# Attention with heads in pairs, a spread and masked forget-gate bias, and attention steps inside the query units, in a float32 decoder of two layers

## The chip, the cores and the metric

The kernel runs on one core of a Trainium2 chip. The metric is the device time of one execution in microseconds (us). The engines are named as the profile names them: PE (matmuls and transpositions; PEld loads its weights), DVE (vector), ACT (scalar, activations), POOL (general) and SP (here only a queue of DMAs).

## The reference, cut to what matters

The model has two layers on 256 tokens of width 1024. Each layer is a half-step feed-forward block (hidden width 2816), a token mixer and a second half-step block. The mixer of layer 0 is a gated linear recurrence, that of layer 1 is attention with a forget gate: keys, values and the gate's running sum `c` come from the stream after layer 0, and there are 16 heads of 64.

```python
kv = (hn @ w_kv).reshape(Bn, S, 2, N_HEADS, HEAD_DIM)
log_f = jax.nn.log_sigmoid((hn @ w_f + b_f).astype(jnp.float32))
c = jnp.cumsum(log_f, axis=1).transpose(0, 2, 1)
...
logits = jnp.einsum('bhqd,bhkd->bhqk', q[:, :, q0:end], k[:, :, :end]).astype(jnp.float32)
logits = logits + c[:, :, q0:end, None] - c[:, :, None, :end]
logits = jnp.where(kpos[None, :] <= qpos[:, None], logits, -jnp.inf)
p = jax.nn.softmax(logits, axis=-1).astype(v.dtype)
outs.append(jnp.einsum('bhqk,bhkd->bhqd', p, v[:, :, :end]))
...
return o @ w_o
```

## The kernel before, in words

**Tokens and weights.** The 256 tokens are two token tiles (t = 0, 1) of 128. Each float32 weight arrives by a DMA on SP's queue as a unit of 128x1024 in one of five `raw` buffers. ACT copies its upper part into `whi` (L199) and DVE subtracts to get the lower part `wlo` (L200). A product is the sum of three matmuls: upper by upper, upper by lower, lower by upper. Either the tokens are stationary and 512 weight columns stream (`mm3`, lines L207, L208, L209), or the weights are stationary and the tokens stream (`mmj`): one matmul of 512 columns, the upper and lower tokens side by side (L222), and one of 256 (L223).

**The order.** PE's instructions run in the order in which the program writes them. The program is a list of items, each with a preparation (load and split) and a piece of work; `slot` runs one, and `tick`, in the middle of each, starts preparations and the calls that `defer(n, fn)` has put off by n ticks. The instructions of ACT, DVE, POOL and SP are put in order by a scheduler, and those traced inside `tc.high_priority()` come ahead of others.

**Banks.** PSUM has eight banks of 512 columns: 0 to 3 for sums ("mm"), 4 and 5 ("gt"), 6 and 7 for transpositions ("tr"). A tile with stationary weights borrows four banks for its eight rows of k (`lent`), in units of two rows (`still`, k0 = 0, 2, 4, 6). At its end `total` and the functions beside it read the four banks (ACT L549, DVE L550).

**Small transpositions.** Gains and parameters are loaded as rows and transposed on PE by deferred calls: `grow` (40 rows, L157) and `prow` (88 rows, L699), each inside a weight-stationary tile of the first feed-forward block.

**K and V.** After layer 0 `v_items` computes V, and `proj_items` K, both with tokens stationary, between 502 and 552 us. `heads_T` (L1010) scales a half of K (`htok`), puts one more column or two behind the 64 of each head (a one and the negative running sum `nck`), and transposes it head by head to `kT` in groups of four heads (L1026), so that a head has 66 rows. Q is treated alike, with the running sum `cq` and a one: the product of the 66 rows then contains the bias of the forget gate. `running` computes the running sums with a triangular matrix.

**Attention.** The string `ATT_ORDER` writes the order of the stage that begins at 736 us: "0" and "1" stand for a unit of token tile 0 or 1 (eight of Q's projection, then eight of the out-projection by `w_o`), "a0" and "a1" for an attention step. A step i has four parts. `logits(i)`: the products of a group of heads (four for t = 0, two for t = 1) into a "gt" bank (L1128), the causal mask added on the diagonal block (L1129), the negative maximum (L1131), and one exponential per head with its sum (L1136). `values(i-3)`: the transposed probabilities `pT` are stationary and 64 columns of `v` stream (L1155). `turn(i-2)`: four transpositions of the probabilities `pe` (L1144), copied to `pT` (L1146). `output`: when eight heads are complete, they are scaled by the inverse sums to `ot` (L1160), transposed (L1168), and split in an upper part `oh` (L1171) and a lower part `ol` (L1172), the stationary operands of the out-projection.

**The end of a token tile.** When the sums of the out-projection are complete, `enter` squares and adds (ACT `junk`, L236), POOL computes the inverse root (L229, L231), and DVE scales by the gain `gb` (L302) and adds to the stream `h` (L306).

## Time and profile before

| | us |
|---|---|
| runs: lowest, median, highest of 3 | 1008.15, 1009.94, 1010.61 |
| the profiled execution's own time | 1007.29 |
| its span in the trace | 1005.6 |
| PE busy | 991.0 (99%) |
| DVE, ACT, POOL busy | 665.3, 566.1, 51.5 |
| projection of V and K | 502 to 552 |
| Q projection, attention, out-projection | 736 to 815 |

The span is the time from the first to the last instruction in the trace. In rows of a timeline the first number is the start and the second the duration; the ends of matmuls are modelled, so what a matmul costs is read from the starts of neighbours. "x4" is a run of four like instructions. In square brackets stands the idle time of the engine ahead of the instruction, and what ended it. In a group the numbers behind the bar are the busy time in us, the mean in ns and the idle time in us.

### The profile page before, as it was taken

How to read it: one execution, taken by the hardware profiler on the slowest of the kernel's cores; microseconds unless marked ns; L12 is line 12 of the kernel's file. 1: busy time of each engine (PE TensorE's matmuls, PEld its weight loads, DVE VectorE, ACT ScalarE, POOL GpSimd, SP SyncE). 2: the span in 40 equal slices, each digit the busy share in tenths (PEclk: the TensorE clock that was granted, in tenths of full speed). 3: DMA queues.
4: the chain of work that ended last, by engine and by line, in shares of the span. 5: the costliest groups of instructions: out<-in, count | busy, mean ns of one | idle time of the engine just before them, and what ended most of it. 6: DMA issues, size and time to landing. Idle time of an engine off the chain costs nothing.

```text
span 1005.6 us, 13910 instructions
## 1 busy us (share of the span) xinstructions
PE 991.0 (99%) x5302; PEld 847.3 (84%) x5302; DVE 665.3 (66%) x768; ACT 566.1 (56%) x742; POOL 51.5 (5%) x113
## 2 busy tenths in 40 slices
PE   8999999999999999999999999999999999999997
PEld 5887888889988888888898888888888888888885
DVE  5877664568998676664695577674477477666642
ACT  5656543559987555543565555553468566555431
POOL 1500000000003000000000000000020020000000
PEclk9999999999999999999999999999999999999999
DMA  6877656565427666545476766655555057665431
GB/s 230 280 263 204 190 161 197 154 181 151 141 78 250 212 188 187 188 158 185 114 227 218 209 191 184 192 189 168 168 168 168 2 188 237 184 199 195 155 121 42
DMA packets 91864, 178.90 MB, mean 178 GB/s; under 512 B 11790, under 2 KB 31318, under 8 KB 91798
## 3 DMA queue, kind: packets, MB, share of 16 engines
q1 hardware_dynamic: 90550, 176.89, 56.8%
q10 hardware_dynamic: 608, 1.06, 0.3%
q8 instruction: 41, 0.67, 0.3%
q0 software_dynamic: 640, 0.07, 0.1%
q14 instruction: 25, 0.20, 0.1%
HBM read 176.95 MB, written 1.05 MB: 177 GB/s over the span
## 4 chain that ended last, share of the span: by engine, by line
PE 70%; issue 21%; ACT 4%; DVE 4%; POOL 1%; DMA 0%; DVEq 0%; POOLq 0%; ACTq 0%
PE pall L222 21%; PE pall L223 11%; PE pall L209 10%; PE pall L208 10%; PE pall L207 10%; PE pall L845 1%; DVE wlo L200 1%; PE pall L214 1%; PE pall L215 1%; PE pall L216 1%; PE pall L1128 1%; ACT junk L236 1%; PE pall L1155 1%; ACT whi L199 1%; PE pall L1026 1%
## 5 line engine op out<-in xcount | busy, mean ns | idle before, releaser
L200 DVE TENSOR_TENSOR wlo<-raw,whi 128x1024 fp32r<-128x1024 f32 (+4 forms) x329 | 394.6, 1206 | 242.3 <-ACT whi L199 241.8
L199 ACT ACTIVATE whi<-raw 128x1024 fp32r<-128x1024 f32 (+4 forms) x329 | 342.1, 1044 | 290.3 <-PE pall L209 125.6
L222 PE MATMUL pall<-xall,whi 128*128 128x512 f32 x1216 | 424.7, 395 | 0.0
L223 PE MATMUL pall<-xall,wlo 128*128 128x256 f32 x1216 | 338.4, 278 | 0.0
L222 PEld LDWEIGHTS pall<-xall,whi 128*128 128x128 f32 x1216 | 228.1, 188 | 53.3
L223 PEld LDWEIGHTS pall<-xall,wlo 128*128 128x128 f32 x1216 | 228.8, 188 | 0.2
L207 PE MATMUL pall<-whi,hhi 128*128 128x512 f32 (+2 forms) x432 | 166.0, 384 | 0.0
L209 PE MATMUL pall<-whi,hlo 128*128 128x512 f32 (+2 forms) x432 | 165.0, 382 | 0.0
L208 PE MATMUL pall<-wlo,hhi 128*128 128x512 f32 (+2 forms) x432 | 164.8, 382 | 0.0
L209 PEld LDWEIGHTS pall<-whi,hlo 128*128 128x128 f32 x432 | 81.1, 188 | 15.1
L208 PEld LDWEIGHTS pall<-wlo,hhi 128*128 128x128 f32 x432 | 81.2, 188 | 14.7
L207 PEld LDWEIGHTS pall<-whi,hhi 128*128 128x128 f32 x432 | 81.2, 188 | 14.6
L207 PE MATMUL pall<-whi,xall 128*128 128x512 f32 (+2 forms) x168 | 67.1, 400 | 0.1
L208 PE MATMUL pall<-wlo,xall 128*128 128x512 f32 (+2 forms) x168 | 64.9, 386 | 0.4 <-DVE wlo L1226 0.2
L209 PE MATMUL pall<-whi,xall 128*128 128x512 f32 (+2 forms) x168 | 64.9, 386 | 0.1
L229 POOL TENSOR_SCALAR nv<-ss 128x1 f32<-128x1 f32 x24 | 10.9, 453 | 749.8 <-ACT junk L236 749.6
L208 PEld LDWEIGHTS pall<-wlo,xall 128*128 128x128 f32 x168 | 31.7, 189 | 7.5 <-DVE wlo L200 1.2
L209 PEld LDWEIGHTS pall<-whi,xall 128*128 128x128 f32 x168 | 31.5, 188 | 7.1 <-DVE xall L259 1.1
L207 PEld LDWEIGHTS pall<-whi,xall 128*128 128x128 f32 x168 | 31.6, 188 | 5.7 <-ACT xall L254 0.5
L567 ACT ACTIVATE hhi<-prod 128x1024 fp32r<-128x1024 f32 (+1 forms) x21 | 20.6, 980 | 25.2 <-DVE prod L563 25.2
L300 DVE SCALAR_TENSOR_TENSOR t<-pall,rstd,gb 128x512 f32<-128x512 f32 x16 | 11.9, 748 | 26.7 <-ACT junk L236 26.7
L557 ACT ACTIVATE sil<-sil 128x1024 f32<-128x1024 f32 (+1 forms) x21 | 20.6, 982 | 15.1 <-DVE sil L556 15.0
(190 smaller groups left out, 974.2 us busy)
## 6 DMA issues: line engine op xcount, KB each, us to landing
raw<-in_ffn_w_down_dram SPq DMA_DIRECT2D x88, 512.0 KB
raw<-in_ffn_w_up_dram SPq DMA_DIRECT2D x80, 512.0 KB
raw<-in_ffn_w_gate_dram SPq DMA_DIRECT2D x79, 512.0 KB
raw<-in_rg_w_in_dram SPq DMA_DIRECT2D x20, 504.0 KB
raw<-in_rg_w_out_dram SPq DMA_DIRECT2D x10, 504.0 KB
raw<-in_ffn_w_gate_dram SPq DMA_DIRECT2D x18, 256.0 KB
raw<-in_ffn_w_up_dram SPq DMA_DIRECT2D x16, 256.0 KB
raw<-in_w_kv_dram SPq DMA_DIRECT2D x8, 512.0 KB
```

Source lines behind the costliest of these rows:

```text
L199: nc.scalar.activation(hi[:parts, c:c + m], rawv[:, c:c + m], AF.Copy)
L200: nc.vector.tensor_tensor(lo[:parts, c:c + m], rawv[:, c:c + m], hi[:parts, c:c + m].bitcast(F32), ALU.subtract)
L207: nc.tensor.matmul(ps, xh, wh, start=first, stop=False)
L208: nc.tensor.matmul(ps, xh, wl, start=False, stop=False)
L209: nc.tensor.matmul(ps, xl, wh, start=False, stop=last)
L214: nc.tensor.matmul(ps, wh, xh, start=first, stop=False)
L222: nc.tensor.matmul(pall[:, b, :], wh, xall[:, k, :, :].rearrange("p a b -> p (a b)"), start=k == 0, stop=False)
L223: nc.tensor.matmul(pall[:, b, :S], wl, xhi[:, k, :], start=False, stop=k == 7)
L229: nc.gpsimd.tensor_scalar(v, ss[:, 0:1], ss[:, 1:2] if n == 2 else 0.0, D * EPS * f * f, ALU.add, ALU.add)
L300: nc.vector.scalar_tensor_tensor(t1[n], pf[n], r_in, gb[:, n * 512:(n + 1) * 512], ALU.mult, ALU.mult)
L557: nc.scalar.activation(s, s, AF.Silu)
L567: nc.scalar.activation(hv, pv, AF.Copy)
```

## The change

**K** becomes a weight-stationary product: `still`, `tile_items` and `total` move to the top level and take the streaming operand as an argument, and the upper and lower halves of `hid` become one tile so that both can stream as one operand. K comes out transposed; its eight groups of transpositions are gone, and a product with the tokens' inverse roots takes their place. `kT` is now [128, 8, 256]: two heads of 64 rows below each other.

**The forget gate** leaves the 66 rows. `nck` is transposed once per token tile (two small transpositions), written to DRAM (`ckd`), and read back by two broadcast loads on SP's queue, `nb0` (1.05 MB) and `nb1` (2.10 MB), to all 128 partitions. POOL writes the causal mask into each (`affine_select` over 2048 elements of a partition). DVE adds this bias to the whole 128x512 logits instead of the mask on the diagonal block.

**The attention step** runs values, turn, logits in this order. Logits use 64 rows of the array per head, the two heads of a pair in its two halves, into two banks. The probabilities are scaled by the inverse sums before they are transposed (one product of 128x512 per group). In `values`, `v` is stationary (64 columns) and 128 columns of `pT` stream; the two heads of a pair write the two halves of the partitions, so the result is transposed already, and `oh` and `ol` are read from it; `ot` and `output` are gone. The vector and scalar operations of the logits stand in `tc.high_priority()`. Q is transposed in four groups of pairs instead of eight of single heads.

**Deferred calls** marked `calm` wait while a weight-stationary tile is in its first or last unit (`state["edge"]`); `ATT_ORDER` is new.

PE at the transposition of `prow`, in the first feed-forward block (`xall` the tokens, `whi` and `wlo` the parts of a weight unit, whose number is that of the build), before:

```order
L222 MATMUL pall<-xall,whi_626 128x512
L223 MATMUL pall<-xall,wlo_627 128x256
L699 MATMUL pall<-ident,prow 126x88
L222 MATMUL pall<-xall,whi_626 128x512
L223 MATMUL pall<-xall,wlo_627 128x256
```

and PE at the same transposition in the changed kernel:

```order
L232 MATMUL pall<-xall,whi_647 128x512
L233 MATMUL pall<-xall,wlo_648 128x256
L712 MATMUL pall<-ident,prow 126x88
L232 MATMUL pall<-xall,whi_647 128x512
L233 MATMUL pall<-xall,wlo_648 128x256
```

It stood behind eight pairs of the first unit of a tile (rows k0 = 0) and stands behind eight pairs of the next unit (k0 = 2), sixteen matmuls later.

PE at the first out-projection unit of token tile 1 (`oh`, `ol` the upper and lower part of the attention's output), before:

```order
L1155 MATMUL pall<-v_2925,pT_6989 128x64
L1155 MATMUL pall<-v_2926,pT_6989 128x64
L1155 MATMUL pall<-v_2925,pT_6989 128x64
L1155 MATMUL pall<-v_2926,pT_6989 128x64
L1144 MATMUL pall<-ident,pe_6962 128x128 x4
L207 MATMUL pall<-whi_6463,oh_6475 128x512
L208 MATMUL pall<-wlo_6464,oh_6475 128x512
L209 MATMUL pall<-whi_6463,ol_6477 128x512
```

and PE there in the changed kernel:

```order
L1202 MATMUL pall<-pT_6904,v_2928 64x128 x2
L1202 MATMUL pall<-pT_6904,v_2929 64x128 x2
L1187 MATMUL pall<-ident,pe_6891 128x128 x4
L1162 MATMUL pall<-kT,qT_6466 128x256 x2
L207 MATMUL pall<-whi_6447,oh_6469 128x512
L208 MATMUL pall<-wlo_6448,oh_6469 128x512
L209 MATMUL pall<-whi_6447,ol_6471 128x512
```

A group of logits has moved from ahead of the values to behind the turn, and the unit follows it; the group's values read the pair's probabilities as streaming operand.

DVE in the changed kernel at the same place: the end of token tile 0 (`t`, `h`) and the logits and `ol` of token tile 1 (`nb` the bias, `mx` the maximum, `sm` the sums):

```order
L312 TENSOR_TENSOR t_1097_6934<-pall,gb_6611 128x512
L1180 RECIPROCAL sm_6911<-sm_6911 128x2
L1181 TENSOR_TENSOR pe_6912<-pe_6912,sm_6911 128x512
L312 TENSOR_TENSOR t_1098_6936<-pall,gb_6611 128x512
L316 SCALAR_TENSOR_TENSOR h_73<-t_1097_6934,rstd_6940,h_73 128x512
L1170 TENSOR_TENSOR pall<-pall,nb_6460 128x2x256
L316 SCALAR_TENSOR_TENSOR h_73<-t_1098_6936,rstd_6940,h_73 128x512
L1172 TENSOR_REDUCE mx_6959<-pall 128x2
L1209 TENSOR_TENSOR ol_6471<-pall,oh_6469 128x512
```

The subtraction that makes the first `ol` of token tile 1, which PE's L209 above reads, stands behind both additions to `h` and a group's bias and maximum.

SP's queue in the changed kernel, ahead of and in the attention stage:

```order
L184 DMA raw_6412<-in_attn_w_q_dram 128x2x512
L187 DMA raw_6445<-in_attn_w_o_dram 128x1024
L187 DMA raw_6594<-in_attn_w_o_dram 128x1024
L187 DMA raw_6613<-in_attn_w_o_dram 128x1024
L1133 DMA nb_6455<-ckd 128x16x128
L1133 DMA nb_6460<-ckd 128x4096
L362 DMA gb_6611<-in_mix_post_g_dram 128x1024
L187 DMA raw_6625<-in_attn_w_o_dram 128x1024
L187 DMA raw_6660<-in_attn_w_o_dram 128x1024
L187 DMA raw_6672<-in_attn_w_o_dram 128x1024
```

The two loads of the bias are new and stand ahead of the gain and of the fourth unit of `w_o`; before, four units of `w_o` stood ahead of the gain and nothing between them.

The diff, cut to its core (in the attention, lines of before that fall away stand in the kernel above):

```diff
-    def defer(n, fn):
-        pend.append([n, fn])
+    def defer(n, fn, calm=False):
+        pend.append([n, fn, calm])
 
     def tick():
         for p in list(pend):
             p[0] -= 1
-            if p[0] < 0:
+            if p[0] < 0 and not (p[2] and state["edge"]):
...
+    def total(v, b, m):
+
+        nc.scalar.activation(v, pall[:, b:b + m, S:], AF.Copy)
+        nc.vector.tensor_tensor(v, pall[:, b:b + m, :S], v, ALU.add)
+
+    def still(u, k0, b0, moving=x_moving):
+        if k0 == 0:
+            assert not set(held) & set(range(b0, b0 + 4)), held.keys()
+            lent.update(range(b0, b0 + 4))
+        state["edge"] = k0 in (0, 6)
+        for j in range(2):
+            for b in range(4):
+                o = j * 512 + b * P
+                mmj(b0 + b, u.hi[:, o:o + P], u.lo[:, o:o + P], k0 + j, moving)
+            if j == 0:
+                tick()
+        if k0 == 6:
+            lent.difference_update(range(b0, b0 + 4))
+            state["edge"] = True
...
-        defer(5, lambda: gains_T(grow, 40, 16))
+        defer(5, lambda: gains_T(grow, 40, 16), True)
...
+    def heads_T(pool, ps, t, n, scale, dst):
+
+        tok = pool.tile([P, 512], F32, tag="htok", name=nm("htok"), bufs=2)
+        nc.vector.tensor_scalar(tok, ps, rs[t][:, 0:1], scale, ALU.mult, ALU.mult)
+
+        def turn():
+            tp = bank("mm")
             for j in range(4):
-                nc.tensor.transpose(tp[:HA, j * P:(j + 1) * P], tok[:, 4 * b + j, :], ident)
-            nc.scalar.activation(dst[:, 8 * n + 4 * b:8 * n + 4 * b + 4, :],
-                                 tp[:HA, :].rearrange("p (a b) -> p a b", a=4), AF.Copy)
-        defer(2, lambda: turn(0))
-        defer(3, lambda: turn(1))
+                nc.tensor.transpose(tp[:, j * P:(j + 1) * P], tok[:, j * P:(j + 1) * P], ident)
+            nc.scalar.activation(dst[:, 4 * n:4 * n + 4, :].rearrange("p a b -> p (a b)"), tp, AF.Copy)
+        defer(2, turn)
 
     def post_k(n):
-        return lambda t, ps: heads_T(pools["f"], ps, t, n, 1.0, (None, kv["nck"][t]), kv["kT"][:, :, t * P:(t + 1) * P])
+        def f(b, m):
+            kk = pools["f"].tile([P, 16 * HA], F32, tag="prod", name=nm("kk"), bufs=1)[:, :1024]
+            v = kk.rearrange("p (a b) -> p a b", a=4)
+            total(v, b, m)
+            nc.vector.tensor_tensor(kv["kT"][:, 4 * n:4 * n + 4, :], v, rcp["v"].unsqueeze(1).to_broadcast([P, 4, S]), ALU.mult)
+        return f
+
+    def z_moving(k):
+        return kv["z"][:, :, :, k, :], kv["z"][:, 0, :, k, :]
...
+    def rows(t):
+        pc = sparebank()
+        nc.tensor.transpose(pc[:NH, :P], kv["nck"][t], ident)
+        nc.vector.tensor_copy(kv["ckT"][:, t * P:(t + 1) * P], pc[:NH, :P])
+        if t == 1:
+            nc.sync.dma_start(kv["dram"], kv["ckT"])
...
-        proj_items(A["w_kv"], n * 512, 512, z_x, post_k(n))
+        tile_items(A["w_kv"], n * 512, 4 - 4 * n, post_k(n), z_moving)
...
+        src = kv["dram"].rearrange("h k -> (h k)").partition_broadcast(P).rearrange("p (h k) -> p h k", h=NH)
+        att["nb"] = []
+        for t in range(2):
+            nb = ap.tile([P, NH, (t + 1) * P], F32, name=f"nb{t}")
+            nc.sync.dma_start(nb, src[:, :, :(t + 1) * P])
+            v = nb[:, :, t * P:]
+            nc.gpsimd.affine_select(out=v, in_=v, compare_op=ALU.is_ge, fill=NEG, base=0,
+                                    pattern=[[0, NH], [-1, P]], channel_multiplier=1)
+            att["nb"].append(nb)
+        att["q"] = [ap.tile([P, 8, P], F32, name=f"qT{t}") for t in range(2)]
...
+        def head(hg, b, j):
+            return 2 * (hg * np_ + j) + b
+
         def logits(hg):
...
+            c = 4 + (hg % 2) * 2
+            lg = pall[:, c:c + 2, :S]
+            for j in range(np_):
+                for b in range(2):
+                    p = hg * np_ + j
+                    nc.tensor.matmul(lg[:, b, j * w:(j + 1) * w], att["q"][t][b * HD:(b + 1) * HD, p, :],
+                                     kv["kT"][b * HD:(b + 1) * HD, p, :w], start=True, stop=True)
+            with tc.high_priority():
+                v = lg.rearrange("p b (j k) -> p j b k", j=np_)
+                h0 = hg * per
+                bias = att["nb"][t][:, h0:h0 + per, :].rearrange("p (j b) k -> p j b k", b=2)
+                if np_ == 1:
+                    v, bias = lg, att["nb"][t][:, h0:h0 + per, :]
+                nc.vector.tensor_tensor(v, v, bias, ALU.add)
+                mx = spool.tile([P, 4], F32, tag="mx", name=nm("mx"))[:, :per]
+                nc.vector.tensor_reduce(mx, lg.rearrange("p b (j k) -> p b j k", j=np_), AX.X, ALU.max, negate=True)
+                sm = spool.tile([P, 4], F32, tag="sm", name=nm("sm"))[:, :per]
+                pe = box["pe", hg] = ap.tile([P, per, w], F32, tag="pe", name=nm("pe"), bufs=2)
+                for b in range(2):
+                    for j in range(np_):
+                        i = b * np_ + j
+                        nc.scalar.activation(pe[:, i, :], lg[:, b, j * w:(j + 1) * w], AF.Exp, bias=mx[:, i:i + 1],
+                                             accum_out=sm[:, i:i + 1])
+                nc.vector.reciprocal(sm, sm)
+                nc.vector.tensor_tensor(pe, pe, sm.unsqueeze(2).to_broadcast([P, per, w]), ALU.mult)
 
         def turn(hg):
...
+            tp = bank("mm", again=True)
             pev = box["pe", hg].rearrange("p a b -> p (a b)")
             for j in range(4):
                 nc.tensor.transpose(tp[:, j * P:(j + 1) * P], pev[:, j * P:(j + 1) * P], ident)
...
+            pT = box["pT", hg] = ap.tile([P, 4, P], F32, tag="pT", name=nm("pT"), bufs=2)
+            with tc.high_priority():
+                nc.scalar.activation(pT.rearrange("p a b -> p (a b)"), tp, AF.Copy)
 
         def values(hg):
...
+            p0 = hg * np_
+            if p0 % 4 == 0:
                 box["po"] = mmbank()
...
+            po, pT = box["po"], box["pT", hg]
+            for j in range(np_):
+                o = (p0 + j) % 4 * P
                 for k in range(nk):
...
+                    for b in range(2):
+                        hd = head(hg, b, j)
+                        nc.tensor.matmul(po[b * HD:(b + 1) * HD, o:o + P], kv["v"][k][:, hd * HD:(hd + 1) * HD],
+                                         pT[:, (b * np_ + j) * nk + k, :], start=k == 0, stop=k == nk - 1)
+            if (p0 + np_) % 4 == 0:
+                b = (p0 + np_) // 4 - 1
+                oh_v = att["oh"][t][:, 4 * b:4 * b + 4, :].rearrange("p a b -> p (a b)")
+                ol_v = att["ol"][t][:, 4 * b:4 * b + 4, :].rearrange("p a b -> p (a b)")
+                nc.scalar.activation(oh_v, po, AF.Copy)
+                nc.vector.tensor_tensor(ol_v, po, oh_v.bitcast(F32), ALU.subtract)
                 release(po)
 
...
         steps = []
...
+        for i in range(G + 3):
             s = []
...
             if 0 <= i - 3 < G:
                 s.append(lambda i=i: values(i - 3))
             if 0 <= i - 2 < G:
                 s.append(lambda i=i: turn(i - 2))
...
+            if i < G:
+                s.append(lambda i=i: logits(i))
             steps.append(s)
...
-    ATT_ORDER = ("0 0 0 0 0 0 0 0 a0 1 a0 1 1 1 a0 1 a0 1 a0 1 a0 a1 1 a0 "
-                 "0 a1 a0 a1 0 a1 0 a1 0 a1 0 a1 0 a1 0 a1 0 a1 1 a1 1 a1 1 1 1 1 1 1")
+    ATT_ORDER = ("0 0 0 0 0 0 0 a0 0 a0 1 1 1 a0 1 1 a0 1 1 a0 1 a1 0 a0 0 a1 0 a0 0 a1 0 a1 0 a1 0 a1 0 a1 1 a1 1 a1 1 a1 1 a1 1 1 1 1")
...
-    defer(40, rg_params)
+    defer(40, rg_params, True)
```

More of the change, by code (lines that the diff above doesn't have):

```diff
@@ L65, in trunk_kernel, with bank @@
     held = {}
-    def bank(kind, hold=False):
-        i = next(i for i in order[kind] if i not in held)
-        assert i not in lent, (kind, i)
+    def bank(kind, hold=False, again=False):
+        free = [i for i in order[kind] if i not in held and i not in lent]
+        i = free[-1 if again else 0]
         order[kind].remove(i)
@@ L1306, in trunk_kernel @@
     run_ffn(ffn_b)
-    run(n_kv)
+    run_ffn((n_v, n_kv, n_kv))
     run_ffn(ffn_c)
```

144 lines of the change are left out of this document (42 added, 102 removed).

## The prediction, put on record before the changed kernel ran

> **What bounds the kernel now.** I read the page's head and its share of busy time first, then the chain that ended last, then PE's list of waits.
>
> ```profile
> span 1005.6 us, 13910 instructions
> PE 991.0 (99%) x5302; PEld 847.3 (84%) x5302; DVE 665.3 (66%) x768; ACT 566.1 (56%) x742; POOL 51.5 (5%) x113
> PE 70%; issue 21%; ACT 4%; DVE 4%; POOL 1%; DMA 0%; DVEq 0%; POOLq 0%; ACTq 0%
> PE pall L699 <- issue: 2.1, 1, 2.1
> ```
>
> PE is busy for 991.0 of 1005.6 us, and 70% of the last chain is PE's own work. So time is won by giving PE fewer instructions or by removing one of its few waits, and lost by a new wait on another engine. The longest wait in the list is the 2.1 us of one transposition at L699 (`prow`). DVE and ACT have a third of the span free on average, but the average says nothing of the attention stage, where they feed PE within a microsecond.
>
> All sums below are made against the profiled execution's own 1007.29 us (its span of 1005.6 and 1.7 around it). The median of the runs shown is 1009.94, 2.65 above, and I add that at the end.
>
> **The deferred transposition of `prow`.** Three views: PE's timeline at the wait, then DVE's at the same time, then PE's at another small transposition, that of `grow`.
>
> ```profile
> 82.58 0.28 PE L223 MATMUL pall<-xall,wlo 128*128 128x256 f32 x1
> 85.00 0.27 PE L699 MATMUL pall<-ident,prow 88*126 88x88 f32 x1 [2.13 <-issue]
> 85.05 0.48 PE L222 MATMUL pall<-xall,whi 128*128 128x512 f32 x1
> 85.38 0.28 PE L223 MATMUL pall<-xall,wlo 128*128 128x256 f32 x1
> ```
>
> ```profile
> 83.68 1.22 DVE L550 TENSOR_TENSOR prod<-pall,prod 128x1024 f32<-128x1024 f32 x1
> ```
>
> ```profile
> 46.15 0.28 PE L223 MATMUL pall<-xall,wlo 128*128 128x256 f32 x1
> 46.36 0.25 PE L157 MATMUL pall<-ident,grow 40*128 40x40 f32 x1
> 46.54 0.49 PE L222 MATMUL pall<-xall,whi 128*128 128x512 f32 x1
> 46.87 0.28 PE L223 MATMUL pall<-xall,wlo 128*128 128x256 f32 x1
> ```
>
> The transposition writes a bank of the tile that has just ended, and DVE's read of those banks ends at 83.68 + 1.22 = 84.90; PE goes on at 85.00. The edit moves it 16 matmuls later, eight pairs of 0.345 us (the K rows below show the pair), 2.8 us. PE would be there at about 82.6 + 2.8 = 85.4, half a microsecond after DVE has ended. **Minus 2.1 us**; PE's list shows no other wait in that stretch that could take its place.
>
> **K with stationary weights.** PE at the last of the eight transpositions of K's heads and at the first weight-stationary pair behind it, with the group of the stage (time from 505 to 565).
>
> ```profile
> 550.41 0.60 PE L1026 MATMUL pall<-ident,htok 128*66 128x128 f32 x4
> 550.76 0.47 PE L207 MATMUL pall<-whi,hhi 128*128 128x512 f32 x1
> 551.08 0.39 PE L208 MATMUL pall<-wlo,hhi 128*128 128x512 f32 x1
> ...
> 552.23 0.40 PE L222 MATMUL pall<-xall,whi 128*128 128x512 f32 x1
> 552.46 0.28 PE L223 MATMUL pall<-xall,wlo 128*128 128x256 f32 x1
> 552.58 0.39 PE L222 MATMUL pall<-xall,whi 128*128 128x512 f32 x1
> ```
>
> ```profile
> L1026 PE MATMUL pall<-ident,htok 128*66 128x128 f32 x32 | 4.8, 272 | 0.0
> ```
>
> One group of four costs 0.35 us to the next start, and the matmul behind it takes 0.32 to its successor where a plain one takes 0.23, so 0.44 in all. The 32 transpositions are eight groups: **minus 3.5 us**. The products change their form but not their columns: the 96 matmuls of 512 columns at 0.23 (22.1 us) become 64 pairs at 0.35 (22.4 us), **plus 0.3**. What is added on ACT and DVE (a copy, an add and a product, each over 128x1024, twice) comes behind the PE work and is read first in the attention, beyond 735 us; the next feed-forward block's matmuls lie over it. Without that cover its price would be some 3 us of DVE and ACT for each half of K.
>
> The forget gate's sums are transposed once more, two small ones. The `grow` rows price one: from 46.15 to 46.87 are 0.72, two plain steps (0.12 and 0.23) are 0.35, so 0.37. Bounds 0.15 (the `prow` rows: 0.05 and 0.10 behind the wait) and 0.37; I take 0.3 each, **plus 0.6**.
>
> **Transpositions of Q and of the output.** Q's eight groups become four (heads in pairs fill 128 partitions): **minus 1.8**. The four groups on `ot` (L1168) vanish, since values now come out transposed: **minus 1.8**, by the same 0.44. The price of both is on other engines: the normalisation moves from `ot` (four products) to `pe` (twelve products of 128x512 and twelve reciprocals on DVE). They lie beside the step's matmuls: a step below lasts 3.55 us (786.14 to 789.69), and DVE has then an add, a reduction and a product at about 0.7 each to do in it, 2.1. If a weight split falls into the same step it is full, and the rest hangs over into the waits priced further down.
>
> **Logits and values.** PE in the steady attention of token tile 1.
>
> ```profile
> 786.14 1.03 PE L1128 MATMUL pall<-kT,qT 66*128 66x256 f32 x4
> 787.00 1.00 PE L1155 MATMUL pall<-v,pT 128*128 128x64 f32 x8
> 787.84 0.61 PE L1144 MATMUL pall<-ident,pe 128*128 128x128 f32 x4
> 788.21 0.48 PE L207 MATMUL pall<-whi,oh 128*128 128x512 f32 x1
> ...
> 789.69 1.03 PE L1128 MATMUL pall<-kT,qT 66*128 66x256 f32 x4
> ```
>
> A group of logits takes 0.86, a group of values 0.84, a transposition of probabilities 0.37. The counts stay (24 groups of logits and values), but each matmul now uses half of the array: 64 rows for logits, 64 columns of output for values, which stream 128 columns instead of 64. That two halves work side by side, no row of before shows. What the rows do show is the price of changing the size: `grow`, with 40 rows, costs 0.37 where `prow`, with 88 rows, costs 0.15 beside its wait, so going into a half array and back costs about 0.22. Bounds for a group: both halves one after the other at the old pace, plus 0.22; both at once, 0.42 less and 0.22 more, minus 0.20. Over 24 groups that is plus 5.3 to **minus 4.8**. I take **0**, half of the overlap, because the four transpositions of 128 columns at 0.37 say that the doubled columns of values cost about as much per instruction as before (0.09 against 0.105), and neither end is nearer to a row.
>
> [...]
>
> **New waits in the attention.** DVE's adds of the bias run over 512 columns, all with priority, and the order of DVE puts the lower half `ol` of the first output block of token tile 1 behind the end of token tile 0's out-projection. PE's third matmul of the unit needs `ol`. Before, the stage had this wait alone.
>
> ```profile
> 796.29 1.10 PE L1155 MATMUL pall<-v,pT 128*128 128x64 f32 x8 [0.31 <-ACT pT L1146]
> ```
>
> It goes: **minus 0.3**. The new chain, from the end of PE's sum for token tile 0 (ACT, POOL and DVE timelines, then groups of DVE from 735 to 810):
>
> ```profile
> 800.70 0.60 ACT L236 ACTIVATE junk<-pall 128x512 bf16<-128x512 f32 x1 [0.68 <-PE pall L209]
> ```
>
> ```profile
> 801.48 0.30 POOL L229 TENSOR_SCALAR nv<-ss 128x1 f32<-128x1 f32 x1 [33.49 <-ACT junk L236]
> 801.86 0.57 POOL L231 TENSOR_TENSOR rstd<-nv,mhalf 128x1 f32<-128x1 f32 x1
> ```
>
> ```profile
> 802.47 1.41 DVE L306 SCALAR_TENSOR_TENSOR h<-t,rstd,h 128x512 f32<-128x512 f32 x2 [0.36 <-POOL rstd L231]
> ```
>
> ```profile
> L1131 DVE TENSOR_REDUCE mx<-pall 128x2 f32<-128x512 f32 x8 | 5.5, 688 | 0.2
> ...
> L1129 DVE TENSOR_TENSOR pall<-pall,cmask 128x512 f32<-128x512 f32 x4 | 2.8, 695 | 1.0 <-PE pall L1128 0.9
> L1172 DVE TENSOR_TENSOR ol<-pall,oh 128x512 fp32r<-128x512 f32 x4 | 2.7, 686 | 0.5 <-ACT oh L1171 0.5
> ```
>
> From the start of `junk` to DVE's `h` are 802.47 - 800.70 = 1.77; then DVE does `h` 0.70, the bias add 0.70, `h` 0.70, the reduction 0.69 and `ol` 0.69, 5.25 in all. PE has beside it values 0.84, a transposition 0.45, logits 0.86 and two matmuls 0.46, together 2.61. **Plus 2.6**, with bounds 0 (DVE free, `ol` done early) and 3.5 (ACT busy with an exponential when the sum ends). The second: after the last values of token tile 1 the next unit needs `oh` and `ol` at once, where the old order had units between. ACT copies in 0.60, DVE subtracts in 0.69, 1.3; PE has two matmuls (0.46) to do before it needs `ol`, and ACT may first be in the middle of a split of weights (rows below):
>
> ```profile
> L200 DVE TENSOR_TENSOR wlo<-raw,whi 128x1024 fp32r<-128x1024 f32 (+4 forms) x329 | 394.6, 1206 | 242.3 <-ACT whi L199 241.8
> L199 ACT ACTIVATE whi<-raw 128x1024 fp32r<-128x1024 f32 (+4 forms) x329 | 342.1, 1044 | 290.3 <-PE pall L209 125.6
> ```
>
> So 0.8 alone and 1.9 behind a split; half a split more than alone, **plus 1.5**. Splits that stand ahead of a logits product in the phase of token tile 0 could add 0 to 1 more; I take none.
>
> **The sum.** -2.1 - 3.5 + 0.3 + 0.6 - 1.8 - 1.8 + 0 - 0.3 + 2.6 + 1.5 = -4.5, or 1002.8 for the profiled execution and **1005.4** beside the median. Forecast by itself: 1003 to 1008.
>
> **The rivals.** First, *the new waits stay away*: DVE is 66% busy, and if the priority brings `ol` forward, 4.1 less: 1001.3. Against it speaks the order, which names `ol` last. Second, *the half tiles run wholly in parallel*: -4.8, so 1000.6. For it speaks that rows or columns of the two halves are disjoint; against it, that no row shows two matmuls overlapping. [...]
>
> Fourth, *POOL and DVE hinder each other* in the two masks over 2048 elements per partition (L1135 of the changed kernel). POOL's timeline shows both prices of a 128-element mask:
>
> ```profile
> 313.14 3.27 POOL L1001 TENSOR_SCALAR_AFFINE_SELECT triu<-triu 128x128 f32<-128x128 f32 x1
> ...
> 317.05 0.29 POOL L1007 TENSOR_SCALAR_AFFINE_SELECT cmask<-cmask 128x128 f32<-128x128 f32 x1
> ```
>
> The same work took 0.29 and 3.27; sixteen times 0.29 is 4.6 for one mask, and if DVE's splits or the first logits wait for one for two thirds of it, +3: 1008.4. [...] Fifth, *`prow` waits again* in its new place, 2.1 more: 1007.5; the margin of half a microsecond speaks against it.
>
> The sixth ends on the slow side: *the bias loads delay the out-projection's weights*. SP's queue now has two broadcast loads (1.05 and 2.10 MB) ahead of the gain and of the fourth to sixth unit of `w_o`. SP's timeline, a window of all engines (its last two numbers are DMA's busy share and GB/s) and the page:
>
> ```profile
> 733.71 3.80 SPq L187 DMA_DIRECT2D raw<-in_attn_w_o_dram  x3
> ```
>
> ```profile
> 742.00:744.50 2.50, 2.50 (x13) 2.07 (x12) 2.50 (x6) 1.23 (x2) 0.96 (x3) 1.00 0.92 320
> ```
>
> ```profile
> DMA packets 91864, 178.90 MB, mean 178 GB/s; under 512 B 11790, under 2 KB 31318, under 8 KB 91798
> ```
>
> The loads can start when the last reads of the old tiles end, at about 737.5. Until the sixth unit they are 3.15 + 0.52 + 1.57 = 5.24 MB: at 320 GB/s 16.4 us, landing at 753.9; at the mean of 178 GB/s 29.4 us, landing at 766.9. The splits of those units stand on ACT ahead of the exponentials of the third group of logits, which PE needs by about 758. Above 758 every microsecond is PE's: at 178 GB/s 767 - 758 = 9 more than the forecast, 1014.4. For it: 512-byte pieces, read 128 times. Against it: the queues are 0.92 busy at 320 GB/s when they have work.
>
> **How the numbers follow.** Chances: forecast 0.42, waits away 0.11, full overlap 0.11, drains 0.14, masks 0.05, `prow` 0.03, bias loads 0.14. The range goes from full overlap with a little of its margin, 999.5, to the drains with theirs, 1012.5; the bias loads and small tails stay out, about 0.18. A measurement of this kernel tells 0.3%, 3.0 us, from no change: faster is under 1006.9, slower above 1013.0. Four fifths of the forecast and both fast rivals are faster (0.56); the rest of the forecast, the drains, the masks and `prow` are the same (0.29); the bias loads and a bad sum of drains and waits are slower (0.15).
>
> **What would show it.** At the changed kernel's transposition of `prow` (L712) no wait; between 505 and 565 us no groups on `htok` and K shorter by 3 us; groups of logits and values at their old 0.85 (0.63 with full overlap, 1.07 with drains); one wait of PE for `ol` (L1209) near the end of token tile 0's out-projection, and one after the last values. I am wrong if PE waits in the first logits for the bias or for `whi` of the out-projection, or if a mask of POOL stands in PE's chain.

## The result, and the profile after

No difference: 1008.92 us (median of 12 runs) against 1008.64 of the kernel before (12), ratio 0.9999, interval 0.9985 to 1.0012, that is -1.5 to +1.2 us. One of the twelve runs, slow at 3282.88 us, is left out of the ratio, and the median of the other eleven is 1008.10. The forecast was -4.5; the likeliest case did not come, though the time lies in the range. The profiled execution took 1008.09, its span is 1006.4 (before 1007.29 and 1005.6). The page and PE's list of waits, after:

```profile
span 1006.4 us, 13846 instructions
PE 986.2 (98%) x5272; PEld 833.0 (83%) x5272; DVE 676.2 (67%) x784; ACT 562.5 (56%) x732; POOL 52.2 (5%) x97
```

```profile
PE pall L209 <- DVE ol L1209: 3.5, 2, 2.9
...
PE pall L207 <- ACT oh L1208: 1.0, 1, 1.0
...
PE pall L207 <- DVE htok L1026: 0.8, 1, 0.8
...
PE pall L1187 <- ACT pe L1178: 0.7, 1, 0.7
...
PE pall L207 <- ACT v L1109: 0.5, 1, 0.5
```

PE is busy for 4.8 us less, and the 2.1 us of `prow` are gone from the list. Seven lines of waits are new, the five shown and two of 0.3 (`qT` and `t`). Laying equal matmuls of both traces over each other gives the account by stage, in us of the two profiled executions:

| stage | after minus before |
|---|---|
| transposition of `prow` | -2.4 |
| rest of the first feed-forward block (to 136) | +1.0 |
| 136 to 513, of it about 0.5 a wait for `v` | +1.0 |
| V and K | -3.1 |
| Q, attention, out-projection | +2.5 |
| last feed-forward block | +1.8 |
| sum, as the spans have it | +0.8 |

**`prow`**, PE after: it follows the pair at once.

```profile
85.33 0.28 PE L233 MATMUL pall<-xall,wlo 128*128 128x256 f32 x1
85.45 0.24 PE L712 MATMUL pall<-ident,prow 88*126 88x88 f32 x1
85.48 0.48 PE L232 MATMUL pall<-xall,whi 128*128 128x512 f32 x1
```

**A steady step** of token tile 1, PE after:

```profile
777.73 0.66 PE L1202 MATMUL pall<-pT,v 128*64 128x128 f32 x8
778.32 0.66 PE L1187 MATMUL pall<-ident,pe 128*128 128x128 f32 x4
778.91 0.70 PE L1162 MATMUL pall<-kT,qT 64*128 64x256 f32 x4
779.54 0.50 PE L207 MATMUL pall<-whi,oh 128*128 128x512 f32 x1
...
781.13 0.66 PE L1202 MATMUL pall<-pT,v 128*64 128x128 f32 x8
```

Values take 0.59 (0.84 before) and logits 0.63 (0.86), but the turn between them 0.59 (0.37) and the unit 1.59 (1.48): the halves gain 0.48, and their full-size neighbours, the turn and the unit, take 0.33 longer. The step is 3.40 against 3.55; over twelve steps that would be -1.8, an estimate from this one.

**The wait for `ol`**, DVE and then PE after:

```profile
790.06 0.75 DVE L316 SCALAR_TENSOR_TENSOR h<-t,rstd,h 128x512 f32<-128x512 f32 x1 [0.25 <-POOL rstd L241]
790.73 0.69 DVE L1170 TENSOR_TENSOR pall<-pall,nb 128x512 f32<-128x512 f32 x1
791.33 0.74 DVE L316 SCALAR_TENSOR_TENSOR h<-t,rstd,h 128x512 f32<-128x512 f32 x1
791.99 0.69 DVE L1172 TENSOR_REDUCE mx<-pall 128x2 f32<-128x512 f32 x1
792.59 0.68 DVE L1209 TENSOR_TENSOR ol<-pall,oh 128x512 fp32r<-128x512 f32 x1
```

```profile
790.04 0.40 PE L208 MATMUL pall<-wlo,oh 128*128 128x512 f32 x1
793.33 0.50 PE L209 MATMUL pall<-whi,ol 128*128 128x512 f32 x1 [2.89 <-DVE ol L1209]
...
794.44 1.11 PE L1202 MATMUL pall<-pT,v 128*64 128x128 f32 x8
795.48 1.11 PE L1187 MATMUL pall<-ident,pe 128*128 128x128 f32 x4
796.53 1.23 PE L1162 MATMUL pall<-kT,qT 64*128 64x256 f32 x4
797.68 0.59 PE L207 MATMUL pall<-whi,oh 128*128 128x512 f32 x1
```

The chain is the one forecast. Behind it the next groups take 1.04, 1.05 and 1.15 instead of 0.59, 0.59 and 0.63. A table of windows says why; the number behind PE's, PEld's, DVE's, ACT's and POOL's busy time is the granted clock:

```profile
795.00:796.00 1.00, 1.00 (x9) 0.67 (x6) 0.53 (x2) 0.61 (x1) 0.00 (x0) 0.50 0.00 0
```

The clock is at half for 3.41 us, 794.5 to 797.9; that cost 1.5 us. The runs behind the result divide by their mean clock: three of the eleven, at 0.999, took 1006.70 to 1006.77, and eight, at 0.992 to 0.997, took 1007.90 to 1011.61.

**Pairs of matmuls.** L222 before and L232 after, counted by windows in PE's column, in the last block:

```profile
850.00:920.00 70.00, 70.00 (x203) 37.88 (x202) 1.00 0.64 190
```

```profile
850.00:920.00 70.00, 70.00 (x199) 37.23 (x199) 1.00 0.63 188
```

203 pairs against 199 in the same 70 us, with the clock at 1.00 in both. From the starts of neighbours, the distance of two pairs is 0.347 us before and 0.353 after. The stream has two rhythms, and the shapes of the matmuls are the same. The slow one is not new: in the second feed-forward block both kernels have 0.353, and in the third both have 0.347.

### The profile page after: what moved, and what is told of

It reads as the page before. It is cut to its first block, busy times and chain, and to the rows that moved or that the text cites. A ratio compares the mean times of both kernels' runs of the same rounds, so it can differ in the third digit from the quotient of the medians.

```text
span 1006.4 us, 13846 instructions
## 1 busy us (share of the span) xinstructions
PE 986.2 (98%) x5272; PEld 833.0 (83%) x5272; DVE 676.2 (67%) x784; ACT 562.5 (56%) x732; POOL 52.2 (5%) x97
## 3 DMA queue, kind: packets, MB, share of 16 engines
q10 hardware_dynamic: 608, 1.06, 0.3%
HBM read 180.09 MB, written 1.06 MB: 180 GB/s over the span
## 4 chain that ended last, share of the span: by engine, by line
PE 67%; issue 22%; ACT 4%; DVE 4%; POOL 1%; DMA 0%; DVEq 0%; ACTq 0%; POOLq 0%
PE pall L232 23%; PE pall L233 12%; PE pall L207 9%; PE pall L209 9%; PE pall L208 9%; DVE wlo L200 1%; PE pall L858 1%; PE pall L214 1%; PE pall L215 1%; PE pall L216 1%; ACT junk L246 1%; ACT whi L199 1%; POOL rstd L241 1%; PE pall L255 1%; DVE h L316 1%
## 5 line engine op out<-in xcount | busy, mean ns | idle before, releaser
L232 PE MATMUL pall<-xall,whi 128*128 128x512 f32 x1216 | 427.2, 397 | 0.0
L232 PEld LDWEIGHTS pall<-xall,whi 128*128 128x128 f32 x1216 | 228.3, 188 | 55.0
L207 PE MATMUL pall<-whi,hid 128*128 128x512 f32 (+2 forms) x400 | 153.1, 383 | 0.5 <-ACT v L1109 0.5
L209 PE MATMUL pall<-whi,hid 128*128 128x512 f32 (+2 forms) x400 | 152.4, 381 | 0.0
L208 PE MATMUL pall<-wlo,hid 128*128 128x512 f32 (+2 forms) x400 | 152.3, 381 | 0.0
L207 PEld LDWEIGHTS pall<-whi,hid 128*128 128x128 f32 x400 | 75.1, 188 | 14.6 <-ACT v L1109 0.8
L209 PEld LDWEIGHTS pall<-whi,hid 128*128 128x128 f32 x400 | 75.1, 188 | 13.8
L208 PEld LDWEIGHTS pall<-wlo,hid 128*128 128x128 f32 x400 | 75.1, 188 | 13.6
L209 PE MATMUL pall<-whi,xall 128*128 128x512 f32 (+2 forms) x168 | 64.9, 386 | 0.1
L209 PEld LDWEIGHTS pall<-whi,xall 128*128 128x128 f32 x168 | 31.5, 188 | 7.1 <-DVE xall L269 1.2
L604 ACT ACTIVATE hid<-prod 128x1024 fp32r<-128x1024 f32 (+1 forms) x21 | 20.6, 981 | 23.1 <-DVE prod L600 23.1
```

The lines of the kernel that those rows point to most:

```text
L207: nc.tensor.matmul(ps, xh, wh, start=first, stop=False)
L208: nc.tensor.matmul(ps, xh, wl, start=False, stop=False)
L209: nc.tensor.matmul(ps, xl, wh, start=False, stop=last)
L232: nc.tensor.matmul(o, wh, both, start=k == 0, stop=False)
L604: nc.scalar.activation(hv, pv, AF.Copy)
```

## The experiments

Ratios are to the kernel before, in runs on the same chip. "Profile" is one execution.

**1. `oh` and `ol` first.** Base: the changed kernel.

```diff
-                nc.scalar.activation(oh_v, po, AF.Copy)
-                nc.vector.tensor_tensor(ol_v, po, oh_v.bitcast(F32), ALU.subtract)
+                with tc.high_priority():
+                    nc.scalar.activation(oh_v, po, AF.Copy)
+                    nc.vector.tensor_tensor(ol_v, po, oh_v.bitcast(F32), ALU.subtract)
```

> The changed kernel with the two operations that make oh and ol from the values also traced with priority; on DVE the first ol of token tile 1 then stands ahead of both additions to h. Theory (a wait that also halves the clock): PE's wait for ol, 2.9 us in the profile of the changed kernel, shrinks to under 0.5, and since PE is then never idle that long, the granted clock stays at 1.0 behind it, where it was 0.5 for 3.4 us and cost 2.6 more. Together about -5.3: some 1003 for the profiled execution, ratio to before about 0.995. Rival (the wait only moves): the additions to h come later by as much, the transposition of h for the next block waits in its place, and the time changes by less than 1 us.

Measured: 0.9953 (0.9940 to 0.9965), median 1004.22, span 1002.5. PE in its profile:

```profile
789.99 0.40 PE L208 MATMUL pall<-wlo,oh 128*128 128x512 f32 x1
790.41 0.50 PE L209 MATMUL pall<-whi,ol 128*128 128x512 f32 x1
...
791.54 0.66 PE L1202 MATMUL pall<-pT,v 128*64 128x128 f32 x8
792.12 0.66 PE L1187 MATMUL pall<-ident,pe 128*128 128x128 f32 x4
792.71 0.70 PE L1162 MATMUL pall<-kT,qT 64*128 64x256 f32 x4
```

The wait is gone, and the groups behind it run at full pace. The span falls by 3.9: 2.9 and 1.5, less 0.5 of a new wait for `pe`. (The 2.6 in the expectation for the half clock was misread; 1.5 is what the groups above give.) The five times lie between 1004.00 and 1004.33, where those before spread over 3 us. No other change of order was needed for the gain of 4.6 us, nor did a later transposition of `h` wait. Part of the evenness is luck: runs 8 and 9 contain the same three lines and spread from 1004.11 to 1007.24, at ratios that mean about 3.5 us less than before. Both of their profiles show the half clock once more, from 804.4 and 805.5 us on (mean clocks 0.997 and 0.998), behind the two waits at the end of the attention, 1.04 and 0.65, which this edit leaves.

**2. The wait filled with matmuls**, and **3. the same, once only** (the first issued them a second time behind the wait, as its operands are asked for twice). Base: the changed kernel.

```diff
+    def parts_of_o(t, k):
+        if t == 1 and k == 0:
+            for _ in range(12):
+                nc.tensor.matmul(pall[:, state["free"], :], att["oh"][0][:, 0, :],
+                                 att["oh"][0][:, :4, :].rearrange("p a b -> p (a b)"), start=True, stop=True)
+        return att["oh"][t][:, k, :], att["ol"][t][:, k, :]
```

> The changed kernel with twelve extra matmuls of 512 columns (about 2.7 us; their sums are not used) ahead of the first out-projection unit of token tile 1, where PE waits 2.9 us for ol; nothing else is changed. Theory (the idle time sets the clock): the wait shrinks to about 0.2, the unit goes on at the same time as before, but the granted clock stays at 1.0, so the values, turn and logits behind it take 0.59, 0.59 and 0.65 again and not 1.04, 1.05 and 1.15: about -2.0 to -2.6. Rival (the half clock comes from the kind of work, not from the idle time): the clock still goes to 0.5 there and the time stays or grows by 0.2.

> The experiment with the filled wait, with its twelve extra matmuls once only (the run before had issued them twice, the second time behind the wait, 2.7 us that nothing hid). Theory (the idle time halves the clock): the granted clock stays at 1.0 in the attention, the unit goes on at the same time, 2.0 to 2.6 less than in an execution of the changed kernel with a dip; over many executions less, since not all of them have one: ratio to before 0.997 to 0.999. Rival (the clock costs nothing that counts): ratio 1.000.

Measured: 1.0012 (1.0003 to 1.0020) and 0.9990 (0.9981 to 0.9998). PE in the profile of the second, and a row of its table of windows:

```profile
794.08 0.66 PE L1203 MATMUL pall<-pT,v 128*64 128x128 f32 x8
794.66 0.65 PE L1188 MATMUL pall<-ident,pe 128*128 128x128 f32 x4
795.25 0.70 PE L1163 MATMUL pall<-kT,qT 64*128 64x256 f32 x4
795.88 0.50 PE L207 MATMUL pall<-whi,oh 128*128 128x512 f32 x1
```

```profile
793.00:797.00 4.00, 4.00 (x25) 2.71 (x26) 2.58 (x4) 2.52 (x6) 1.02 (x3) 1.00 0.01 2
```

In neither profile does PE's list name a wait for this `ol`, and the groups behind take 0.58 to 0.63 with the clock at 1.00; the second filling cost the first of the two runs 2.7. So the half clock at this place comes from PE's idle time, not from the kind of work. (In run 3 it comes later instead, from 807.5 us on, behind the same two waits at the end as in runs 8 and 9; the mean clock of this execution is 0.996.) The size on the mean, about 1 us against the changed kernel, is at the edge of what these runs tell.

**4. `prow` in its old place.** Base: the changed kernel.

```diff
-    defer(40, rg_params, True)
+    defer(40, rg_params)
```

> The changed kernel with the transposition of prow back in its old place, behind eight pairs of the first unit of the tile. Both theories: PE waits there for about 2.1 us as before. Theory (a transposition that does not wait throws the stream of pairs into a slower rhythm): behind it the pairs take 0.347 again and not 0.353, so that until the end of the first feed-forward stage 1.0 us comes back and the edit costs 1.1 in all: about 1009.2. Rival (the slower rhythm is a property of the streaming operand's new form): pairs stay at 0.353, and the edit costs 2.1: about 1010.2.

Measured: 1.0029 (1.0016 to 1.0042). PE waits 2.1 again, and here the half clock follows that wait, too (mean clock 0.994, against 0.996 in the changed kernel's profile). Pairs in the rest of the first block, counted as above, in this run and in the changed kernel:

```profile
93.00:130.00 37.00, 37.00 (x108) 19.98 (x107) 1.00 0.61 191
```

```profile
93.00:130.00 37.00, 37.00 (x106) 19.63 (x106) 1.00 0.63 198
```

Here the pairs take 0.347 behind the transposition, as they do ahead of it, and in the changed kernel 0.353: about 1.1 us came back, as the first theory had it. In the profile the edit costs 2.1 for the wait and 1.6 for the half clock, less that 1.1. As a rule the theory fails: in the profiles of runs 1, 2, 3, 7, 8, 11 and 12 the same transposition, without a wait, turns slow pairs into fast ones.

**5. The kernel before, once more.** No edit.

> The kernel before once more, for its profile. In the first profile its pairs of matmuls with stationary weights ran at 0.347 us in the first and the last feed-forward block, in the profiles of the changed kernel mostly at 0.353, 2.8 us over both blocks. Theory (each execution falls into one rhythm or the other at a break of the stream): this profile shows 0.353 for a part of those blocks, and the kernel before takes up to 2 us more in it than in the first. Rival (the slower rhythm belongs to the changed code): 0.347 in both blocks again.

Measured: 1.0001 (0.9992 to 1.0011); the profiled execution took 1009.50, its span is 1007.8. The pairs are fast in both blocks: the theory of chance by execution fell for the last block. Of the 2.2 us more than in the first profile, 0.6 arise in the first 12 us of the program. What the other 1.6 are, PE's timeline and the windows say (columns as above):

```profile
85.59 0.35 PE L699 MATMUL pall<-ident,prow 88*126 88x88 f32 x1 [2.14 <-issue]
85.66 0.77 PE L222 MATMUL pall<-xall,whi 128*128 128x512 f32 x1
86.23 0.41 PE L223 MATMUL pall<-xall,wlo 128*128 128x256 f32 x1
86.45 0.63 PE L222 MATMUL pall<-xall,whi 128*128 128x512 f32 x1
```

```profile
86.00:88.00 2.00, 2.00 (x7) 1.71 (x7) 1.21 (x4) 1.16 (x2) 0.00 (x0) 0.50 0.86 274
```

Behind the same wait of 2.1 the clock was halved in this execution and not in the first: a pair takes 0.64. The runs of before beside experiment 1 divide in the same way: 13 with a mean clock of 0.998 or more took 1006.98 to 1008.58, 14 with less took 1008.83 to 1010.28. The 15 beside run 12 divide as cleanly; beside runs 5 and 10 the two groups overlap, so the mean clock is not the whole of the spread.

**6. Halves in turn.** Base: the changed kernel; in `logits` and `values` the loop over the half b is put outside.

```diff
-            for j in range(np_):
-                for b in range(2):
+            for b in range(2):
+                for j in range(np_):
```

> The changed kernel with the matmuls of logits and values in another order: first all of the one half of the array, then all of the other, instead of in turns. Theory (two matmuls run at once when they follow each other in different halves): a group of values goes from 0.59 to between 0.8 and 1.05, a group of logits of token tile 0 from 0.65 to about 0.9; that of token tile 1 has only one product for each half and stays. 12 x 0.3 + 4 x 0.25 = about +4.6. [...]

Measured: 1.0004 (0.9993 to 1.0016); all groups within 0.01 of the changed kernel. The order does not matter, which left open whether the halves overlap at all.

**7. One half only.** Base: the changed kernel; the logits of the second head of each pair are left out.

```diff
-                    nc.tensor.matmul(lg[:, b, j * w:(j + 1) * w], att["q"][t][b * HD:(b + 1) * HD, p, :],
-                                     kv["kT"][b * HD:(b + 1) * HD, p, :w], start=True, stop=True)
+                    nc.tensor.matmul(lg[:, b, j * w:(j + 1) * w], att["q"][t][:HD, p, :],
+                                     kv["kT"][:HD, p, :w], start=True, stop=True)
```

> The changed kernel with all logits computed from the first head of each pair, so that every product uses the same half of the array's rows (the second head's logits are left out, the first head's are computed twice). Theory (the two halves run at once): a group goes from 0.63 (token tile 1) and 0.65 (token tile 0) to about 1.06 and 1.07, twelve groups, +5. Rival (a half tile is quicker by itself): both stay within 0.05.

Measured, one execution: 1012.03. A group of token tile 1:

```profile
777.50 1.13 PE L1162 MATMUL pall<-kT,qT 64*128 64x256 f32 x4
778.56 0.50 PE L207 MATMUL pall<-whi,oh 128*128 128x512 f32 x1
```

1.06 instead of 0.63: the halves of the logits do run at once, and as run 6 left the groups as they were, in the one order as in the other. For the values, which use the halves of the columns, no run tests it; that they fell from 0.84 to 0.59 fits.

**8. An extra transposition** in the second and the last feed-forward block, and **9. the same two pairs later** (there `flip` only sets a counter that the unit's loop counts down). Base: experiment 1.

```diff
+    def flip():
+        tp = sparebank()
+        nc.tensor.transpose(tp[:126, :88], ident[:88, :126], ident[:88, :88])
...
+    defer(30, flip, True)
     run_ffn(ffn_d, 5)
```

> The version with oh and ol first (ratio 0.9953), with one extra transposition of 88 columns (its result is not used) in the middle of a unit early in the second and in the last feed-forward block, where all profiles of changed kernels show pairs at 0.353. In five profiles a transposition of 88 columns alone has changed the rhythm from 0.347 to 0.353 or back. Theory (a single transposition shifts the stream's phase by a fixed step): behind it both blocks run at 0.347, about 1.8 us less each, 0.2 for each transposition: some -3.2, ratio about 0.992. Rival (chance): one block or none changes, ratio 0.9935 to 0.996.

> The run with an extra transposition in the second and the last feed-forward block, with that transposition two pairs later in its unit. In the slow rhythm the steps from the first to the second matmul of a pair repeat every three pairs (0.233, 0.241, 0.236); prow, which turned slow into fast in five profiles, came behind 0.241 each time, the extra transposition behind 0.236, and changed nothing. Theory (the place in those three decides): behind 0.241 both blocks turn to 0.347; -1.6 each against the run before, about 1001.5 in the profile, ratio about 0.993. Rival (the place does not decide): pairs stay at 0.353, ratio 0.9955 to 0.9965.

Measured: 0.9965 (0.9954 to 0.9977) and 0.9964 (0.9951 to 0.9977), no faster than their base, and the pairs stay at 0.353 in both blocks. Their profiles are 1.6 and 2.2 us longer than their base's, of which one half clock (run 1) is 1.6. In these blocks a transposition of `prow`'s shape does not set the rhythm, at either of two places; both theories fell.

**10. `prow` alone.** Base: the kernel before, with `calm` for `rg_params` only.

```diff
-    defer(40, rg_params)
+    defer(40, rg_params, True)
```

> The kernel before with one part of the change alone: the transposition of prow waits for the middle of a tile and lands sixteen matmuls later. Theory (the wait of 2.1 us goes, and with it the dip of the clock that follows it in a part of the executions; but the transposition that no longer waits comes at a place of the stream's rhythm where it turns 0.347 into 0.353): -2.1 for the wait, about -1 for the dips, +1.0 for the slower pairs behind it; ratio 0.9975 to 0.9985. Rival (the last feed-forward block's slow rhythm comes from this part as well, through a shift of the program): ratio 0.9995, with pairs at 0.353 behind 840 us.

Measured: 0.9977 (0.9966 to 0.9987), median 1006.40; eight times between 1005.70 and 1006.87. This part alone is worth 2.3 us: the wait and the half clock that can follow it, less slow pairs, which stood in all of the first block of this execution. In the last block they are fast.

**11. The tail of the attention.** Base: experiment 1; one unit of token tile 1 moved behind the last values (the end of `ATT_ORDER`), and priority for `htok`.

```diff
-... 0 a1 0 a1 1 a1 1 a1 1 a1 1 a1 1 1 1 1")
+... 0 a1 0 a1 1 a1 1 a1 a1 1 a1 1 1 1 1 1")
```

> The version with oh and ol first, with two edits against PE's smaller waits in the attention: one out-projection unit of token tile 1 is moved from between two of its last attention steps to behind the last values, and the scaling of Q (htok) is traced with priority. Theory (these waits are chains of ACT and DVE that one unit of PE work covers, 1.4 us): the waits for oh (1.0) and ol (0.6) and that for htok (0.8) go, and with the first two a dip of the clock in some executions: -2.0 to -3, ratio 0.9925 to 0.9935. Rival (the probabilities' copies become the wait where two steps stand side by side): half of it comes back, ratio 0.994 to 0.995.

Measured: 0.9952 (0.9939 to 0.9966), the same as experiment 1. The waits for `oh` and `ol` at the end went, and one of 1.0 for `pT` came where two steps stand side by side, with half clock behind it in this profile (mean clock 0.996, against 0.998 in that of run 1). `htok` still costs 0.8. The rival was nearer.

**12. No priority.** Base: the changed kernel; both `tc.high_priority()` in `logits` and `turn` taken away.

```diff
-            with tc.high_priority():
+            if True:
                 v = lg.rearrange("p b (j k) -> p j b k", j=np_)
```

> The changed kernel without the priority of the logits' operations and of the copies of the probabilities; the order of PE is unchanged. On DVE the first ol of token tile 1 then stands behind both additions to h, but ahead of the next bias and maximum; in the phase of token tile 0 two weight splits stand ahead of a group's bias, maximum and sums. [...]

Measured: 0.9964 (0.9951 to 0.9977), median 1005.08. The wait for `ol` is 1.7 instead of 2.9, and the waits for `pe` and `htok` (1.5 together) do not come at all; new ones of about 0.5 for another `ol` and 0.3 for `pT` do. So it was the priority that cost about 3.5 us. The waits of this profile account for 1.9 of it, 1.2 of them because the bias and the maximum no longer stand ahead of the subtraction that PE needs. The rest is not resolved; eight of these ten runs have a mean clock of 0.998 or more, against three of eleven of the changed kernel, so rarer half clock is the likely cause.

## Why the prediction was wrong in size

Its sum was -4.5 for the profiled execution, and the spans say +0.8. The terms that it named come out near the forecast or below it. What makes most of the difference are three things that it put at nothing: smaller waits, the clock and the rhythm of the pairs. That the time lies in the range is luck: the upper end was put there for halves that run one after the other, which did not happen.

- **`prow`, -2.1:** right in the profile (-2.4), alone worth 2.3 on the mean (run 10).
- **K and the small transpositions, -2.6:** -3.1, with 0.5 of a wait for `v` ahead of it that had no term. (The group at 550.41 that the prediction calls the last of K's eight is the sixth; two more stand at 555.05 and 556.90, at the same cost.)
- **Q and output, -3.6:** not measured alone. PE's trace has eight groups on `htok` and four on `ot` in this stage before, and four on `htok` after, as forecast; -3.6 is what closes the account of the attention with the terms below.
- **Logits and values, 0:** about -1.8. Run 7 shows that both halves run at once in the logits, and the step shows the gain of 0.48 and the price of 0.33. The bounds (-4.8 to +5.3) held it. The case that the chances call "drains" puts a price on each change of size: no run shows that the array drains there. In its place the runs show 0.63 for a group of logits, 1.06 with one half alone, and neighbours that take longer, the turn 0.59 against 0.37 and the unit 1.59 against 1.48.
- **New waits, 4.1:** the two named cost 2.9 (2.6 forecast) and 1.7 (1.5). Others of 0.8, 0.7, 0.3 and 0.3, together 2.1, were not seen. The first two are DVE behind weight splits in the phase of token tile 0, where the prediction had bounds of 0 to 1 and took none.
- **No term for the clock:** the failed step that the runs show best. The prediction priced waits by their length. Behind the wait of 2.9 the clock stood at half for 3.4 us, which cost 1.5 more, and behind that of 2.1 in runs 4 and 5, where it cost 1.6. The half clock came in the profile of the changed kernel and, by the mean clocks, in about half of the executions of the kernel before (14 of 27 beside run 1). The profiled one had none, so the 2.65 from profile to median was not a constant, either. That it is the idle time is shown by runs 1, 2 and 3.
- **No term for the rhythm of the pairs:** +1.0 and +1.8, the largest of the three in this profile. All eleven profiles of kernels with the new attention have slow pairs in the last block, all three with the old one fast pairs. In the first block the rhythm changes at `prow`'s transposition in ten of the eleven profiles in which it does not wait (three times to slow, seven times to fast; in run 10 it stays slow), and in none of the three in which it waits 2.1. What decides it stays open: it is not the matmuls' shapes, and an extra transposition in two other blocks changed nothing (runs 8 and 9).

For the attention: -3.6 (transpositions) - 1.8 (halves) + 6.4 (new waits 6.7, less the old 0.3) + 1.5 (clock) = +2.5, which is what the trace has, though the -3.6 and the -1.8 were not measured apart. In all, beside the forecast: `prow` -0.3, K -0.5, halves -1.8, named waits +0.5, unseen waits +2.1, clock +1.5, rhythm +2.8, and +1.0 between 136 and 513; together +5.3, from -4.5 to +0.8. The rivals with the bias loads and the masks played no part: no wait of PE names `nb`, and the masks took 2.2 and 2.0 us on POOL; that POOL and DVE hinder each other is shown by no run. Halves one after the other, with a price at each change of size, did not come either: the neighbours pay 0.33 a step, but the halves gain more, 0.48.

## What to carry to other kernels

Priority for one chain was a delay for another user of that engine here, about 3.5 us in run 12: look for what PE needs next and stands behind it. Three lines in experiment 1 turned a change without effect into one of -3.5 to -4.6 us. In a kernel like this one, count a half clock, 1.5 to 1.6 us here, as a possible part of the price of PE's waits of 2 us or more: it came behind the 2.9 of the changed kernel, and behind the same 2.1 in two profiles of three (runs 4 and 5, not the first of the kernel before). And don't take one profiled execution for the median when its clock differs from the others'.

## What the runs showed of the hardware

The trace of the changed kernel has one stretch of half clock inside the stages: 3.413 us from 794.49 us on, 1.16 us behind the end of the wait of 2.89. In the second profile of the kernel before (run 5) the clock is 0.91, 0.50 and 0.74 in the three windows of 2 us from 84 to 90 us, 3.4 us at half in all, behind the wait of 2.14. In the first profile the same wait is 2.13, and the clock is 1.00 from 82 to 92 us. The waits of 1.04 and 0.65 at the end of the attention were followed by half clock in the profiles of runs 3, 8 and 9; in that of the changed kernel the clock is 1.00 there, from 806 to 816 us. So waits of equal length came with half clock and without, and what decides between the two is not shown here.

In the trace of the changed kernel the half-size matmuls of logits and values start in twos, 6 to 7 ns apart. Where one half is issued first (run 6) they still start in twos, 13 ns apart where a half has more than one product; the trace does not say which is which. With one half alone (run 7) they start singly, 0.11 and 0.22 us apart.
